# A gated attention block on one core: modulation weights in row pieces after x, v's scale through DRAM, k projected before q

## The chip, the core and the metric

One core of a Trainium2 chip runs the whole kernel. The metric is the device time of one launch in microseconds, as the median of the runs. The engines are TensorE (PE, with its weight loads PEld), VectorE (DVE), ScalarE (ACT), GpSimd (POOL) and SyncE (SP), which only issues transfers here.

## What is computed

```python
mod = c @ w_ada + b_ada                       # shift, scale, gate: 3 x 1024
h = rmsnorm(x, norm_g) * (1 + scale) + shift  # x is 1024 x 1024 float32
proj = h @ w_in                               # q, k, v, z of A and of B, forget logits, two gates
y_a = stick_breaking(q_a, k_a, v_a)           # 8 heads of 64
y_b = forgetting_attention(q_b, k_b, v_b, F)  # 8 heads of 64, F = cumsum(log_sigmoid(f))
y = g0 * ((y_a * silu(z_a)) @ w_o_sb) + g1 * ((y_b * silu(z_b)) @ w_o_fox)
out = rmsnorm(x + gate * (y @ w_out), final_g)
```

## The kernel before

Every float32 product is made of three fp32r matmuls on a high and a low part (`mm3`, lines 181 to 183). A value is split into the two parts by `split` (line 163): ScalarE copies the high part (L165) and VectorE, or GpSimd for some, subtracts it (L166).

**The start** (lines 196 to 332). A list of tokens, `SEQ`, gives the program order: X loads a tile of 128 rows of x, L loads modulation weights, R loads a weight of the first four projections, s squares a tile of x, n makes the inverse norms, x scales and transposes a tile (a tile in `DIAG` is scaled by a matmul with a diagonal matrix, the others by VectorE; `CPY` says who evacuates each bank), a weighs the modulation weights with c (`weigh`), f turns them into the factors of one group of 128 channels (`factors`), m modulates and splits that group (`modulate`), w splits a weight, p projects that group into seven accumulators: two halves of q, of k and of a gate, and one half of z. A scheduler orders each engine's instructions when the program is built, with `SEQ` as the priority, so the order on an engine isn't always that of the list. `load_ada` loads, for a channel group, all 1024 rows of 128 columns of shift and of scale (256 for groups 3 and 4), so a row of a transfer has 512 bytes, and one piece is enough for `factors` of its group. The buffers `ada1`, `ada1b` and `xb1` are reused, `xb1` after x has left it. The splits of the four first weights subtract on GpSimd (`POOLW`).

**The attention stages.** Pairs p = 0 to 7 have two heads each (0 to 3 mixer A, 4 to 7 mixer B), j = 0, 1. `attention(p, j)` runs 12 ticks over row blocks: scores (L623, L625 with `kx`, a copy of k with high and low part swapped that GpSimd's queue moves by DMA, L404 and L405), logits (L701, L708, L713), exponentials (ACT), a DMA transpose of the weights (L663), then products with v (L756, L757) into one `pv` bank that VectorE reduces (L765) and GpSimd scales (L766). Score tiles and the small transposes (`tp_tile`) share one ring of four banks. In mixer B, GpSimd also masks the diagonal block of the bias (L696) before L713 reads it.

**The filler.** Between these, PE gets the projections still needed, as units of 8 steps of three matmuls (v units in steps of six narrower ones). `plan[p, 0]` and `plan[p, 1]` list the units for the two heads of pair p: z of p, gates, v of the next two pairs, and `proj_qk(p + 1)`, q first and then k. `sprinkle` calls small jobs after a counted number of steps. `residual_gate` (18 jobs, one every six steps over pairs 4 and 5) loads and weighs the remaining third of `w_ada` on VectorE (L599).

**v's scale.** For each two pairs of v, `largest` transposes the maxima of the 128 partitions on PE (L467), takes the maximum and makes two powers of two on one partition (L469 to L475); `spread` broadcasts them with a small matmul (L480) and copies them out (L482); `take_v` scales v to 16-bit parts. `forget_gates` (L571) transposes the forget logits through a ring bank at the end of `plan[2, 0]`.

Of the kernel before, what the change touches and what calls it, by code (L numbers as in the profile page):

```python
# [18 lines left out]
P = 128  # L19
# [10 lines left out]
FP = 2  # L30
PEK = ()
EVACS = "k0 z0 g0 g1 q0 k1 q1"
# [4 lines left out]
POOLX = ()  # L37
DIAG = (1, 4, 6)
POOLW = (0, 1, 2, 3)
BATCH = (4,)  # L40
CPY = "dd aa aa aa ad dd ad aa"
GROUPS = ((0,), (1,), (2,), (3, 4), (5,), (6,), (7,))
ADATAG = ("ada1", "ada1b", "ada1", "ada2", "xb1", "ada1b", "ada1")
SEQ = "X2 L0 X0 s0 X1 X3 X4 s3 a0 X7 s2 X6 X5 s1 n0 x0 L1 s4 s5 s7 s6 R0 L2 x2 f0 R2 L3 n1 x1 a3 a1 x3 x4 R1 w0 x5 f1 x7 x6 R3 m0l w1l L6 w1r m0r m1l m1r a2 w3l L5 w2 f2 a5 f3 m2 m3l a6 p0l p1l f4 p0r w3r p1r m3r f5 p2l L7 f6 m4 m5l p2r p3l p3r a7 f7 m6 m5r m7l p4 p5 p6l p6r m7r p7"
WPOOL = ()
# [12 lines left out]
PVAT = (18, 16, 14, 10)  # L58
PVFIRST = 12
TURNAT = (22, 20, 18, 14)  # L60
# [8 lines left out]
def tile_hybrid_block(ctx, tc, x, c, w_ada, b_ada, norm_g, w_in, b_forget,  # L69
# [19 lines left out]
    vd = [dram.tile([P, S], F32, name=f"vd{i}") for i in range(8)]  # L89

    fd = dram.tile([8, S], F32, name="fd")
    gated = dram.tile([1, D], F32, name="gated")
# [5 lines left out]
    def tp_tile():  # L98
        return ps_z.tile([P, 512], F32, name="tp", tag="ps")
# [59 lines left out]
    def load_raw(src, shape, name="wraw"):  # L159
        raw = wpool.tile(shape, F32, name=name, tag="wraw", bufs=3)  # L160
        nc.sync.dma_start(raw, src)
        return raw

    def split(hi, lo, raw, pool=False):
        nc.scalar.copy(hi, raw)  # L165
        (nc.gpsimd if pool else nc.vector).tensor_sub(lo, raw, hi)  # L166
        return hi, lo
# [29 lines left out]
    with tc.tile_pool(name="start", bufs=1) as sp:  # L197
# [4 lines left out]
        half = {"": slice(0, S), "l": slice(0, 512), "r": slice(512, S)}  # L202
        group = {k: g for g in GROUPS for k in g}
        edges = (0,) + BATCH + (TB,)
# [6 lines left out]

        def load_ada(k):
            n = len(group[k]) * P
            tag = ADATAG[GROUPS.index(group[k])]
            ada = sp.tile([P, KB, 2, n], F32, name="ada", tag=tag, bufs=1)
            for j in range(2):
                nc.sync.dma_start(ada[:, :, j, :],
                                  wada[:, j * D + k * P: j * D + k * P + n].rearrange("(q p) n -> p q n", p=P))
            adas[k] = ada

# [51 lines left out]

        def weigh(k):

            n = len(group[k]) * P
            if k in PEK:
                return
            o = ams[k] = sp.tile([P, 2, n], F32, name="am", tag="am%d" % n, bufs=2)
            nc.vector.tensor_scalar(o, adas[k][:, 0], cT[:, 0:1], None, ALU.mult)
            for q in range(1, KB):  # L280
                nc.vector.scalar_tensor_tensor(o, adas[k][:, q], cT[:, q:q + 1], o, ALU.mult, ALU.add)

        def factors(k):
            k0 = group[k][0]
            pm = acc_tile(2)
            for j in range(2):
                if k in PEK:
                    for q in range(KB):
                        nc.tensor.matmul(pm[:, j:j + 1], adas[k][:, q, j, :], cT[:, q:q + 1], start=q == 0,
                                         stop=q == KB - 1)  # L290
                    continue
                nc.tensor.matmul(pm[:, j:j + 1], ams[k0][:, j, (k - k0) * P:(k - k0 + 1) * P], ones,
                                 start=True, stop=True)
            nc.vector.tensor_add(ashf[:, k:k + 1], pm[:, 0:1], b_shift[:, k:k + 1])
            nc.vector.scalar_tensor_tensor(amul[:, k:k + 1], pm[:, 1:2], b_scale1[:, k:k + 1], gT[:, k:k + 1],
                                           ALU.add, ALU.mult)
# [152 lines left out]
    def qcol(p):  # L449
        return (QA if p < 4 else QB) + (p % 4) * P  # L450

    def proj_qk(p):
        return proj(qcol(p), evac_q, p) + proj(qcol(p) + 512, evac_k, p)

# [4 lines left out]
    vmost = {}  # L459
    ones_row = rows[0:1, :]  # L460
    nc.vector.memset(ones_row, 1.0)

    def largest(p):


        pt = tp_tile()
        nc.tensor.transpose(pt[0:1, :P], vmost[p], ident)  # L467
        top = at.tile([1, 1], F32, name="vtop", tag="vtop", bufs=2)
        nc.vector.tensor_reduce(top, pt[0:1, :P], mybir.AxisListType.X, ALU.max)  # L469
        nc.vector.tensor_scalar(top, top, 1e-25, None, ALU.max)  # L470
        e = top.bitcast(I32)
        nc.vector.tensor_scalar(e, e, 0x7F800000, None, ALU.bitwise_and)
        pair = vscale[p] = at.tile([1, 2], F32, name="vpow", tag="vpow", bufs=2)
        nc.vector.tensor_scalar(pair[:, 0:1].bitcast(I32), e, -1.0, float((254 + VSCALE) << 23), ALU.mult, ALU.add)
        nc.vector.tensor_scalar(pair[:, 1:2].bitcast(I32), e, 1.0, float((VSCALE + 15) << 23), ALU.mult, ALU.subtract)  # L475

    def spread(p):

        pt = tp_tile()
        nc.tensor.matmul(pt[:, 0:2], ones_row, vscale[p], start=True, stop=True)  # L480
        o = at.tile([P, 2], F32, name="vsc", tag="vsc", bufs=2)
        nc.vector.tensor_copy(o, pt[:, 0:2])  # L482
        for q in (p, p + 1):
            vscale[q], vback[q] = o[:, 0:1], o[:, 1:2]
# [66 lines left out]
    def load_v(p):  # L551
        vraw[p] = load_raw(vd[p], [P, S], "vraw").rearrange("p (a b d) -> p a b d", a=TB, b=2)
# [16 lines left out]
    def forget_gates():  # L569
        pt = tp_tile()  # L570
        nc.tensor.transpose(pt[:64, :P], fT[0].rearrange("p h a -> p (h a)"), ident)  # L571
# [422 lines left out]
    first_v = proj_v(0)  # L994
    first_v[0].preload()
    def start_evacs():
# [25 lines left out]
    gs = [proj_g(j) for j in list(range(9, 16)) + list(range(8))]  # L1022
    plan = {}
    for p in range(7):
        a, b = [], []
        if p == 0:
            g = sprinkle(gs.pop(0), [(6, lambda: load_v(0)), (8, lambda: largest(0)), (10, lambda: spread(0)),
                                     (13, lambda: take_v(0))])
            a += first_v + g
            vunit[0] = g[1]  # L1030
        else:
            a += proj_z(p)
            zunit[p] = a[-1]
        for _ in range(GSH[p][0]):
            a += gs.pop(0)
        if p % 2:
            a += proj_v(p + 1)
        if p == 2:
            a.append(once(forget_gates))
        b += proj_qk(p + 1)  # L1040
        q = p + 1
        marks = [(14, lambda q=q: largest(q)), (19, lambda q=q: spread(q))] if p % 2 else []
        sprinkle(b, [(12, lambda q=q: load_v(q))] + marks + [(24, lambda q=q: take_v(q))])
        if p == 6:
            a += b[:2]
            b[:2] = []
            b += proj_z(7)
            zunit[7] = b[-1]
        for _ in range(GSH[p][1]):
            b += gs.pop(0)  # L1050
        plan[p, 0], plan[p, 1] = a, b
# [97 lines left out]
```

## Time and profile before

| | |
|---|---|
| device time, 3 runs | 942.94, 944.57, 949.04 us; median 944.57 |
| profiled execution | 944.57 us, of which the span of the core is 942.9 us |
| PE busy | 891.2 us (95% of the span) |
| DVE busy | 704.8 us (75%) |
| ACT busy | 598.3 us (63%) |
| POOL busy | 115.8 us (12%) |
| moved by DMA | 152.14 MB, mean 161 GB/s |

Busy time is taken from one execution. Spans of matmuls overlap, so the distance from one start to the next is what a matmul costs. In a timeline, a bracket holds the idle time of the engine ahead of the row and what ended it. "PEclk" in a table by stretches is the clock granted to TensorE as a share of full speed (2.4 GHz); 0.5 is the lower level.

### The profile page before, as it was taken

Reading aid. Unit: us, or ns where it says so; the run is one execution under the profiler, and the core shown is the slowest. Engines: PE = TensorE matmul, PEld = TensorE weight load, DVE = VectorE, ACT = ScalarE, POOL = GpSimd, SP = SyncE. Lnnn points to the kernel's source line nnn. Section 1 sums busy time; section 2 is a strip of 40 time slices with the busy share of each in tenths; the row PEclk is TensorE's granted clock in tenths of the full one; section 3 lists DMA queues with packets and bytes.
Section 4 is the critical chain, followed back from the end, with each engine's and each line's share of the span. In section 5 each row is a group of like instructions: output and inputs, shape, how many; then the busy total and the mean of one; then the engine's idle time right before and its main releaser. Section 6 shows DMA issues by size and latency. Waiting matters only on the chain. (4 is left out here: it accounts for less than half of the span.)

```text
span 942.9 us, 14905 instructions
## 1 busy us (share of the span) xinstructions
PE 891.2 (95%) x5282; PEld 753.0 (80%) x5282; DVE 704.8 (75%) x1402; ACT 598.3 (63%) x1102; POOL 115.8 (12%) x191
## 2 busy tenths in 40 slices
PE   2799999999999989999999999999999999999997
PEld 2688978889788868889878787897887777788886
DVE  4984998688786788878798768657687767776544
ACT  5656787776777697897678765445667456553222
POOL 0401001000010000100000112211212212540000
PEclk9999999999999989999999999999999999999999
DMA  9933495544594564936548697967999999552221
GB/s 313 305 98 101 100 225 122 127 104 121 132 193 121 143 152 112 176 82 133 147 121 187 175 211 157 210 160 188 192 203 173 279 263 213 201 178 90 101 92 54
DMA packets 260659, 152.14 MB, mean 161 GB/s; under 512 B 157156, under 2 KB 241748, under 8 KB 260584
## 3 DMA queue, kind: packets, MB, share of 16 engines
q1 hardware_dynamic: 257592, 142.78, 60.5%
q0 software_dynamic: 2880, 8.39, 4.9%
q8 instruction: 41, 0.67, 0.3%
q14 instruction: 34, 0.28, 0.1%
q10 hardware_dynamic: 112, 0.02, 0.0%
HBM read 80.31 MB, written 24.71 MB: 111 GB/s over the span
## 5 line engine op out<-in xcount | busy, mean ns | idle before, releaser
L181 PE MATMUL acc<-hhi,w 128*128 128x512 f32 x584 | 237.4, 406 | 0.0
L183 PE MATMUL acc<-hhi,w 128*128 128x512 f32 x584 | 230.0, 394 | 0.0
L182 PE MATMUL acc<-hlo,w 128*128 128x512 f32 x584 | 229.7, 393 | 0.0
L183 PEld LDWEIGHTS acc<-hhi,w 128*128 128x128 f32 x584 | 110.8, 190 | 24.6
L726 DVE SCALAR_TENSOR_TENSOR pc<-pw,pc 128x1024 f16<-128x1024 f32 (+7 forms) x128 | 96.6, 758 | 43.2 <-ACT pc L722 42.4
L181 PEld LDWEIGHTS acc<-hhi,w 128*128 128x128 f32 x584 | 111.4, 191 | 21.7 <-issue 2.0
L182 PEld LDWEIGHTS acc<-hlo,w 128*128 128x128 f32 x584 | 111.3, 191 | 19.6
L722 ACT ACTIVATE pc<-pw 128x1024 f16<-128x1024 f32 (+7 forms) x128 | 86.8, 679 | 19.2 <-DMA wT<-pc 17.8
L718 ACT ACTIVATE pw<-pw,low 128x1024 f32<-128x1024 f32 (+3 forms) x64 | 49.6, 776 | 73.3 <-DVE low L713 73.3
L766 POOL TENSOR_TENSOR ysb<-ysb,fac 128x128 f32<-128x128 f32 x64 | 35.6, 556 | 452.1 <-DVE ysb L765 388.1
L720 ACT ACTIVATE pw<-pw,low 128x1024 f32<-128x1024 f32 (+3 forms) x64 | 49.5, 774 | 62.1 <-DVE low L713 61.7
L530 PE MATMUL acc<-wv,hhi 128*128 128x256 f32 (+1 forms) x256 | 73.6, 288 | 0.0
L532 PE MATMUL acc<-wv,hlo 128*128 128x256 f32 (+1 forms) x256 | 72.4, 283 | 0.0
L531 PE MATMUL acc<-wv,hhi 128*128 128x256 f32 (+1 forms) x256 | 72.4, 283 | 0.0
L701 DVE SCALAR_TENSOR_TENSOR pw<-z,pw 128x512 f32<-128x512 f32 (+4 forms) x96 | 52.9, 553 | 23.1 <-ACT pw L692 22.6
L756 PE MATMUL pv<-vv,wT 128*128 128x128 f16 x534 | 66.6, 220 | 3.7 <-DVE ysb L765 3.7
L623 PE MATMUL z<-ks,qs 128*128 128x512 f32 (+1 forms) x192 | 66.4, 346 | 2.7 <-DVE yT L778 2.7
L625 PE MATMUL z<-kx,qs 128*128 128x512 f32 (+1 forms) x192 | 65.7, 344 | 3.4 <-DMA kx<-ks 3.4
L757 PE MATMUL pv<-vv,wT 128*128 128x128 f16 x534 | 66.5, 220 | 0.0
L166 DVE TENSOR_TENSOR w<-wraw,w 128x1024 fp32r<-128x1024 f32 x44 | 54.0, 1227 | 10.0 <-ACT w L165 8.8
L757 PEld LDWEIGHTS <-wT 128*128 128x128 f16 x576 | 56.6, 98 | 4.4 <-issue 4.1
L708 DVE TENSOR_TENSOR_SCAN pw<-pw 128x512 f32<-128x512 f32 (+2 forms) x64 | 58.9, 921 | 1.2
(276 smaller groups left out, 1985.8 us busy)
## 6 DMA issues: line engine op xcount, KB each, us to landing
wraw<-in_w_in_dram SPq DMA_DIRECT2D x48, 512.0 KB, 4.7
gd<-stg SPq DMA_DIRECT2D x32, 256.0 KB, 2.6
kx<-ks POOLq DMA_DIRECT2D x28, 256.0 KB, 6.4
ada<-in_w_ada_dram SPq DMA_DIRECT2D x12, 512.0 KB, 7.6
zd<-stg SPq DMA_DIRECT2D x16, 256.0 KB, 2.8
zt<-zd SPq DMA_DIRECT2D x32, 128.0 KB, 2.7
vraw<-vd SPq DMA_DIRECT2D x8, 512.0 KB, 3.9
fb<-fd SPq DMA_DIRECT2D x8, 512.0 KB, 4.6
```

The source lines that it names most:

```text
L181: nc.tensor.matmul(ps, w[0], x[0], start=first, stop=False)
L182: nc.tensor.matmul(ps, w[0], x[1], start=False, stop=False)
L183: nc.tensor.matmul(ps, w[1], x[0], start=False, stop=last)
L530: nc.tensor.matmul(ps[:, a], hhi[k][:, t], hi[:, k, :], start=k == 0, stop=False)
L531: nc.tensor.matmul(ps[:, a], hhi[k][:, t], lo[:, k, :], start=False, stop=False)
L532: nc.tensor.matmul(ps[:, a], hlo[k][:, t], hi[:, k, :], start=False, stop=k == KB - 1)
L623: nc.tensor.matmul(o, qs[p, j][:, tq], ks[p, j][:, s], start=True, stop=False)
L625: nc.tensor.matmul(o, qs[p, j][:, tq], kx[p, j][:, s], start=False, stop=not mask)
L722: nc.scalar.activation(pair.parts(a)[0], w, AF.Copy, scale=WSCALE)
L726: nc.vector.scalar_tensor_tensor(lo, pair.logits(a), WSCALE, hi, ALU.mult, ALU.subtract)
L756: nc.tensor.matmul(y[:, a, :], w[:, b + s, :], v, start=s == 0, stop=False)
L757: nc.tensor.matmul(y[:, a, :], w[:, b + nb + s, :], v, start=False, stop=s == nb - 1)
```

## The change

Modulation weights are loaded in eight pieces of 256 rows and 512 columns of shift and of scale (rows of 2048 bytes), four pieces per half of the channels, through three buffers of one tag, all behind the eight tiles of x; `weigh` adds two row groups of 1024 elements per piece, and `factors` of a group needs the four pieces of its half. Five tiles of x instead of three are scaled by a diagonal matmul, fourteen of sixteen transposed banks instead of ten are evacuated by ScalarE, and the four first weight splits subtract on VectorE instead of GpSimd. The splits of v's first weights are put behind the start's last split. v's maxima go through DRAM: GpSimd's queue writes 128 values and reads them back as a row on every partition, and VectorE then makes the powers on all partitions. k is projected ahead of q; the z of pairs 5 and 6 moves from the first half of its own pair to the second half of pair 4 and of pair 5; the first half of pair 6 is left with k of pair 7 and the v jobs, and its second half holds q of pair 7 and, as before, z of pair 7. The forget logits are transposed through the `pv` bank at step 42 of 64.

```diff
-DIAG = (1, 4, 6)
-POOLW = (0, 1, 2, 3)
+DIAG = (1, 4, 5, 6, 7)
+POOLW = ()
-CPY = "dd aa aa aa ad dd ad aa"
-GROUPS = ((0,), (1,), (2,), (3, 4), (5,), (6,), (7,))
-ADATAG = ("ada1", "ada1b", "ada1", "ada2", "xb1", "ada1b", "ada1")
-SEQ = "X2 L0 X0 s0 X1 X3 X4 s3 a0 X7 s2 X6 X5 s1 n0 x0 L1 s4 s5 s7 s6 R0 L2 x2 f0 R2 L3 n1 x1 a3 a1 x3 x4 R1 w0 x5 f1 x7 x6 R3 m0l w1l L6 w1r m0r m1l m1r a2 w3l L5 w2 f2 a5 f3 m2 m3l a6 p0l p1l f4 p0r w3r p1r m3r f5 p2l L7 f6 m4 m5l p2r p3l p3r a7 f7 m6 m5r m7l p4 p5 p6l p6r m7r p7"
+CPY = "dd aa aa aa aa aa aa aa"
+SEQ = "X2 X0 s0 X1 X3 X4 s3 X7 s2 X6 X5 s1 L0 L1 n0 x0 L2 s4 s5 s7 s6 a0 x2 L3 R0 n1 x1 a1 x3 x4 R1 a2 L4 w0 x5 x7 x6 a3 R2 L5 f0 m0l w1l f1 w1r m0r m1l m1r f2 R3 a4 L6 w2 f3 m2 m3l w3l p0l p1l a5 L7 p0r w3r p1r m3r p2l a6 a7 f4 f5 p2r p3l p3r f6 f7 m4 m5l m6 m5r m7l p4 p5 p6l p6r m7r p7"
-PVFIRST = 12
+PVFIRST = 13
...
+    vm = [dram.tile([1, P], F32, name=f"vm{i}") for i in range(4)]
...
+        def load_ada(i):
+
+            ada = adas[i] = sp.tile([P, 2, 2, 512], F32, name="ada", tag="ada", bufs=3)
+            rows_ = wada[i % 4 * 2 * P:(i % 4 + 1) * 2 * P, :]
             for j in range(2):
+                c0 = j * D + i // 4 * 512
+                nc.sync.dma_start(ada[:, :, j, :], rows_[:, c0:c0 + 512].rearrange("(q p) n -> p q n", p=P))
...
+        def weigh(i):
+
+            g = i // 4
+            if i % 4 == 0:
+                ams[g] = sp.tile([P, 2, 512], F32, name="am", tag="am", bufs=2)
+            for x in range(2):
+                q = i % 4 * 2 + x
+                if q == 0:
+                    nc.vector.tensor_scalar(ams[g], adas[i][:, x], cT[:, 0:1], None, ALU.mult)
+                else:
+                    nc.vector.scalar_tensor_tensor(ams[g], adas[i][:, x], cT[:, q:q + 1], ams[g], ALU.mult, ALU.add)
...
-        return proj(qcol(p), evac_q, p) + proj(qcol(p) + 512, evac_k, p)
+        return proj(qcol(p) + 512, evac_k, p) + proj(qcol(p), evac_q, p)
...
     def largest(p):
...
+        nc.gpsimd.dma_start(vm[p // 2].rearrange("o p -> p o"), vmost[p])
+        every = vscale[p] = at.tile([P, P], F32, name="vev", tag="vev")
+        nc.gpsimd.dma_start(every, vm[p // 2].to_broadcast((P, P)))
+
+    def spread(p):
...
+        o = at.tile([P, 3], F32, name="vsc", tag="vsc", bufs=2)
+        top = o[:, 2:3]
+        nc.vector.tensor_reduce(top, vscale[p], mybir.AxisListType.X, ALU.max)
...
     def forget_gates():
-        pt = tp_tile()
+        pt = pv_tile()
...
-    first_v[0].preload()
+    with tc.issue_after(last_split[0].ins), tc.issue_after(last_split[1].ins):
+        first_v[0].preload()
...
-            g = sprinkle(gs.pop(0), [(6, lambda: load_v(0)), (8, lambda: largest(0)), (10, lambda: spread(0)),
-                                     (13, lambda: take_v(0))])
+            g = sprinkle(gs.pop(0), [(4, lambda: load_v(0)), (5, lambda: largest(0)), (13, lambda: spread(0)),
+                                     (14, lambda: take_v(0))])
...
-        else:
-            a += proj_z(p)
-            zunit[p] = a[-1]
+        elif p < 5:
+            a += project_z(p)
...
-            a.append(once(forget_gates))
-        b += proj_qk(p + 1)
+            sprinkle(a, [(42, forget_gates)])
+        if p < 6:
+            b += proj_qk(p + 1)
+        else:
+            qk = proj_qk(7)
+            a += qk[:2]
+            b += qk[2:]
         q = p + 1
-        marks = [(14, lambda q=q: largest(q)), (19, lambda q=q: spread(q))] if p % 2 else []
-        sprinkle(b, [(12, lambda q=q: load_v(q))] + marks + [(24, lambda q=q: take_v(q))])
-        if p == 6:
-            a += b[:2]
-            b[:2] = []
-            b += proj_z(7)
-            zunit[7] = b[-1]
+        marks = [(6, lambda q=q: largest(q)), (20, lambda q=q: spread(q))] if p % 2 else []
+        sprinkle(b if p < 6 else a, marks + [(12 if p < 6 else 5, lambda q=q: load_v(q)), (24 if p < 6 else 14, lambda q=q: take_v(q))])
+        for x in {4: (5,), 5: (6,), 6: (7,)}.get(p, ()):
+            b += project_z(x)
```

## Rows read from the trace of the kernel before

**Rows 1.** The page: span, and busy time and share by engine.

```profile
span 942.9 us, 14905 instructions
...
PE 891.2 (95%) x5282; PEld 753.0 (80%) x5282; DVE 704.8 (75%) x1402; ACT 598.3 (63%) x1102; POOL 115.8 (12%) x191
```

**Rows 2.** Waits, whole span: waiter <- releaser, total us, times, longest.

```profile
PE acc L292 <- DVE am L281: 7.3, 3, 4.5
...
PE tp L480 <- DVE vpow L475: 4.1, 3, 2.2
...
PE pv L756 <- DVE ysb L765: 3.7, 2, 2.0
...
PE z L625 <- DMA kx<-ks: 3.4, 1, 3.4
...
PE z L623 <- DVE yT L778: 2.7, 1, 2.7
...
DVE pw L713 <- POOL fb L696: 4.0, 8, 1.9
```

**Rows 3.** Stretches: length; busy PE, PEld, DVE, ACT, POOL; PEclk; DMA share; GB/s.

```profile
42.20:79.00 36.80, 36.80 (x167) 30.75 (x168) 25.99 (x53) 17.14 (x22) 1.85 (x1) 0.95 0.41 102
...
340.00:350.00 10.00, 7.15 (x51) 5.74 (x49) 8.96 (x19) 8.58 (x20) 0.65 (x1) 0.83 0.65 184
350.00:360.00 10.00, 10.00 (x38) 7.83 (x38) 5.00 (x12) 8.81 (x19) 0.00 (x0) 0.82 0.74 152
...
556.00:591.00 35.00, 30.39 (x191) 25.32 (x189) 26.88 (x51) 19.15 (x34) 7.61 (x15) 1.00 0.79 168
...
590.00:600.00 10.00, 8.52 (x48) 7.17 (x49) 4.43 (x13) 2.62 (x8) 1.45 (x4) 0.83 1.17 255
...
667.00:697.00 30.00, 30.00 (x195) 25.71 (x195) 22.02 (x54) 19.71 (x37) 5.61 (x14) 1.00 0.98 213
```

**Rows 4.** Timeline of PE, the start: start us, us, instruction, idle before.

```profile
30.96 0.48 PE L181 MATMUL z<-hhi,wqk 128*128 128x512 f32 x1
...
42.18 0.61 PE L292 MATMUL acc<-ones,am 128*128 128x1 f32 x4 [2.21 <-DVE am L281]
...
48.90 0.50 PE L292 MATMUL acc<-ones,am 128*128 128x1 f32 x4
49.26 0.48 PE L181 MATMUL pv<-hhi,w 128*128 128x512 f32 x1
...
70.20 0.39 PE L181 MATMUL z<-hhi,wqk 128*128 128x512 f32 x1
...
79.04 0.39 PE L181 MATMUL acc<-hhi,w 128*128 128x512 f32 x1
```

**Rows 5.** Transfers at 8 to 16 us (x), then 16 to 26 us (weights).

```profile
DMA packets 897, 3.28 MB, mean 410 GB/s; under 512 B 96, under 2 KB 96, under 8 KB 897
...
DMA packets 5634, 2.96 MB, mean 296 GB/s; under 512 B 96, under 2 KB 5599, under 8 KB 5634
```

**Rows 6.** DVE's groups by shape: start (first three), whole span (last).

```profile
L281 DVE SCALAR_TENSOR_TENSOR am<-ada,cols,am 128x256 f32<-128x256 f32 x42 | 20.9, 518 | 0.5
...
L281 DVE SCALAR_TENSOR_TENSOR am<-ada,cols,am 128x512 f32<-128x512 f32 x7 | 7.2, 1022 | 0.1
...
L259 DVE TENSOR_SCALAR diag<-ident,inv 128x128 f32<-128x128 f32 x3 | 3.0, 984 | 0.0
...
L599 DVE SCALAR_TENSOR_TENSOR gacc<-wraw,cols,gacc 128x1024 f32<-128x1024 f32 x7 | 9.0, 1282 | 10.7 <-DMA wraw<-in_w_ada_dram 10.7
```

**Rows 7.** Tile kx, all its transfers from GpSimd's queue.

```profile
DMA to landing us min/median/max: 2.2/5.1/8.8
```

**Rows 8.** Timeline of PE at three idle times of the attention stages.

```profile
347.18 0.58 PE L623 MATMUL z<-ks,qs 128*128 128x256 f32 x1 [2.67 <-DVE yT L778]
...
566.78 0.22 PE L756 MATMUL pv<-vv,wT 128*128 128x128 f16 x1 [1.74 <-DVE ysb L765]
...
591.48 0.47 PE L625 MATMUL z<-kx,qs 128*128 128x512 f32 x1 [3.35 <-DMA kx<-ks]
```

More of the change, by code (lines that the diff above doesn't have):

```diff
@@ L30 @@
 FP = 2
-PEK = ()
 EVACS = "k0 z0 g0 g1 q0 k1 q1"
@@ L162, in load_raw @@
         return raw
+    last_split = []
     def split(hi, lo, raw, pool=False):
-        nc.scalar.copy(hi, raw)
-        (nc.gpsimd if pool else nc.vector).tensor_sub(lo, raw, hi)
+        last_split[:] = [nc.scalar.copy(hi, raw), (nc.gpsimd if pool else nc.vector).tensor_sub(lo, raw, hi)]
         return hi, lo
@@ L202, in tile_hybrid_block @@
         half = {"": slice(0, S), "l": slice(0, 512), "r": slice(512, S)}
-        group = {k: g for g in GROUPS for k in g}
         edges = (0,) + BATCH + (TB,)
@@ L210, in load_x @@
             nc.sync.dma_start(xt[t], x2[t * P:(t + 1) * P, :])
[L212 to L215, printed above, removed]
+        def load_ada(i):
+            ada = adas[i] = sp.tile([P, 2, 2, 512], F32, name="ada", tag="ada", bufs=3)
+            rows_ = wada[i % 4 * 2 * P:(i % 4 + 1) * 2 * P, :]
             for j in range(2):
-                nc.sync.dma_start(ada[:, :, j, :],
-                                  wada[:, j * D + k * P: j * D + k * P + n].rearrange("(q p) n -> p q n", p=P))
-            adas[k] = ada
+                c0 = j * D + i // 4 * 512
+                nc.sync.dma_start(ada[:, :, j, :], rows_[:, c0:c0 + 512].rearrange("(q p) n -> p q n", p=P))
         def load_w0(i):
@@ L271, in turn_x @@
                 copy(xnT[:, 4 * b:4 * b + 4, t * P:(t + 1) * P], pt.rearrange("p (a b) -> p a b", a=4))
[L273 to L281, printed above, removed]
+        def weigh(i):
[8 more added lines that the diff above has]
+                    nc.vector.scalar_tensor_tensor(ams[g], adas[i][:, x], cT[:, q:q + 1], ams[g], ALU.mult, ALU.add)
         def factors(k):
-            k0 = group[k][0]
             pm = acc_tile(2)
             for j in range(2):
[L287 to L292, printed above, removed]
+                nc.tensor.matmul(pm[:, j:j + 1], ams[k // 4][:, j, k % 4 * P:(k % 4 + 1) * P], ones,
                                  start=True, stop=True)
@@ L459, in tile_hybrid_block @@
     vmost = {}
-    ones_row = rows[0:1, :]
-    nc.vector.memset(ones_row, 1.0)
     def largest(p):
-        pt = tp_tile()
-        nc.tensor.transpose(pt[0:1, :P], vmost[p], ident)
-        top = at.tile([1, 1], F32, name="vtop", tag="vtop", bufs=2)
-        nc.vector.tensor_reduce(top, pt[0:1, :P], mybir.AxisListType.X, ALU.max)
+        nc.gpsimd.dma_start(vm[p // 2].rearrange("o p -> p o"), vmost[p])
[5 more added lines that the diff above has]
+        nc.vector.tensor_reduce(top, vscale[p], mybir.AxisListType.X, ALU.max)
         nc.vector.tensor_scalar(top, top, 1e-25, None, ALU.max)
@@ L472, in largest @@
         nc.vector.tensor_scalar(e, e, 0x7F800000, None, ALU.bitwise_and)
[L473 to L482, printed above, removed]
+        nc.vector.tensor_scalar(o[:, 0:1].bitcast(I32), e, -1.0, float((254 + VSCALE) << 23), ALU.mult, ALU.add)
+        nc.vector.tensor_scalar(o[:, 1:2].bitcast(I32), e, 1.0, float((VSCALE + 15) << 23), ALU.mult, ALU.subtract)
         for q in (p, p + 1):
@@ L569, in forget_gates @@
     def forget_gates():
-        pt = tp_tile()
+        pt = pv_tile()
         nc.tensor.transpose(pt[:64, :P], fT[0].rearrange("p h a -> p (h a)"), ident)
@@ L1023, in tile_hybrid_block, with project_z @@
     plan = {}
+    def project_z(p):
+        units = proj_z(p)
+        zunit[p] = units[-1]
+        return units
     for p in range(7):
```

## The prediction

> **What bounds the kernel now.** I read the page first. PE is busy 891.2 of 942.9 us, DVE 704.8, ACT 598.3 [rows 1], so TensorE sets the time, and a change can only win where PE stands still or runs at its lower clock. The list of waits, cut to PE, says where: at L292 for the modulation sums (7.3 us, of which 2.2 at 40 us), at L480 for v's powers (4.1), at L756 for the reduction of the single `pv` bank (3.7), at L625 for `kx` (3.4), at L623 for a bank of the score ring (2.7) [rows 2]. The table by stretches adds the second price of a stall: behind those at 347 and 591 us the granted clock is 0.82 to 0.83 over ten microseconds [rows 3, 8]; at half speed that costs 10 x (0.17 + 0.18) = 3.5 us behind the first and 10 x 0.17 = 1.7 us behind the other. Last the start's timeline: from 42.18 us on PE never stops until the first projections end at 79 us, and before that it did little of them [rows 3, 4].
>
> **The start: -5.5 us.** The seven accumulators need 7 x 8 x 3 = 168 matmuls. Their distance is (79.04 - 70.20) / 39 = 0.227 us [rows 4], so 38.1 us in all. Behind 42.2 us stand 143 of them: the stretch has 167 records, 24 of these from six factor groups [rows 3]. Only 25 ran between 30.96 and 42.2, since channel groups came one by one. Where they run without a break, the end is first matmul + 38.1 + eight factor groups of 49.26 - 48.90 = 0.36 [rows 4], 2.9, + one spell of the low clock as now, 0.05 x 36.8 = 1.8 [rows 3]: first + 42.8.
>
> When can the first one run? x moves at 410 GB/s, weights in rows of 512 bytes at 296 [rows 5]; rows of 2048 bytes are not in the trace. I bound them by these two and take the middle, 350, as they lie between both in length. Without the 1.05 MB of modulation weights that now go in among x, its last tile lands some 1.05/0.35 = 3 us earlier than the 16 us at which that rate changes [rows 5]: 13 us. Four pieces (4.19 MB) take 12.0, so 25.0. Behind the last come two sums of 1024 elements, 1.28 each by the nearest row of that shape (L599) [rows 6], then matmul, factors, modulation and split, for which I estimate 3.1: 30.7 us. The first half of the channels then gives 84 matmuls: 84 x 0.227 + 1.4 + 1.8 = 22.3 us of work, to 53.0. The second half needs another 4.19 MB at 350 and 2.1 MB of first weights at 296: 25.0 + 12.0 + 7.1 + 5.7 = 49.8. No gap, and the end is 30.7 + 42.8 = 73.5 against 79.0: -5.5. At 410 for the pieces it is 71.7 (-7.3), at 296 75.7 (-3.3). I keep 0 as the upper end, since the scheduler may order DVE otherwise.
>
> DVE has room. The weighing is 56 instructions now (eight per loaded group), 20.9 + 7.2 us in its two main forms; sixteen of 1.28 are 20.5 [rows 6]. The four subtractions that come over from GpSimd cost about as much each (5.1), and the wider instructions pay for them. DVE also shows slow spells while GpSimd subtracts: a diagonal matrix of 128 elements takes 0.98 us in the mean, where a sum of 256 elements takes 0.52 [rows 6]. Page "SBUF — State Buffer" of the Trainium skill (section "Who interferes with whom") says that a GpSimd instruction and a DVE one with two SBUF inputs block each other whole; by that rule the slow spells go with `POOLW`. The trace fits it, and no term of the sum rests on it. More copies and casts on ACT lie beside PE's 38 us of matmuls; without that cover four copies would be some 2 us. The splits of v's first weights move behind the last split, which should now be done about ten microseconds before PE ends; without that slack they are four passes, some 5 us late.
>
> **v's scale: -4.1 + 1.5.** The two PE steps per pair of pairs and their wait go: -4.1 [rows 2], at best that and at worst nothing, if PE meets the same late DVE at the next `pv` or score bank. New is a chain on GpSimd's queue: a write, its landing, a read, its landing, then six small DVE instructions in place of six. Nearest for a landing is kx's from the same queue: 2.2 to 8.8, median 5.1 [rows 7]. Two make 10.2 (4.4 to 17.6). The cover is 8 steps at pair 0 and 14 later; a step is three matmuls, 0.68 us, and with attention's share about 0.9: 7 us and 13 us. So the median is 3 us late once and in time three times. DVE would stand there and ACT's scaling of v behind it; PE sees part: I take +1.5. The ends are 0 and (17.6 - 7) + 3 x (17.6 - 13) = +24. Behind the write, GpSimd's queue also holds the diagonal masks of mixer B and the scaling of `ysb`; L713 waits for masks 4.0 us in all today [rows 2], once in the change (pair 5) that could grow by a landing, which is inside the 24.
>
> **k before q: -5.1.** The 3.35 us at 591.48 go [rows 8], for `kx` now has q's 16 steps (and z's 16) between its transfer and its use, 11 us or more against a landing of 8.8 at most [rows 7]; with the clock's 1.7 that makes 5.1. Next in line is q, which needs no transfer. At worst the clock falls elsewhere: -3.4.
>
> **z one stage earlier: -1.7 + 3.0.** The second half of pair 4 (556 to 591 us) has 32 steps and PE idles 4.6 us in it; 1.74 of that is the `pv` wait at 566.78 [rows 3, 8]. It gets 48 steps, which should cover that (0 to -3.6, of which I take the 1.7). The steps come from the first halves of pairs 5 and 6. The latter (667 to 697 us) now has PE full for 30.0 us, DVE 22.0, ACT 19.7 [rows 3]. With 16 of 32 steps gone PE needs 30.0 - 10.9 = 19.1. DVE loses two gate multiplications per half of z and a split, some 4 us: 18.0. In the stretch at 556 DVE got through 26.9 us in 35.0, a share of 0.77 [rows 3]; at that share 18.0 takes 23.4 and PE idles 4.3. The ends are 0 and 4.3; I take 3.0, nearer the second, for this is the same kind of stage with a thin filler.
>
> **Forget logits: -4.6.** At 344 to 347 us PE waits 2.85 for ring banks (10 - 7.15) [rows 3], 2.67 of it for a bank that the late L778 holds [rows 8]. The job leaves the ring, so the next score tile gets another bank, and at step 42 of 64 no product with v is due. -2.85, and of the clock's 3.5 I take half. Ends -6.4 and 0. `PVFIRST` one tick later costs nothing: filler covers it, or one tick of about 3 us if not.
>
> **Sum.** -5.5 - 4.1 + 1.5 - 5.1 - 1.7 + 3.0 - 4.6 = -16.5. The profiled execution took 944.57 us and is the median run itself, with a span of 942.9; 944.57 - 16.5 = **928.1 us**.
>
> **Rivals.**
> 1. *The start wins, the middle gives back.* DVE at 75% [rows 1] is why the powers, the `pv` reduction and L778 were late; take one wait away and PE meets the next. For it: three of the four waits behind the start name DVE [rows 2]. Against: they are few, and PE is full for long stretches between. Then only the start, `kx` and the added costs count: -5.5 - 5.1 + 4.5 = -6.1, 938.5 us.
> 2. *The start wins nothing.* Nothing can be projected until four pieces have come; if DVE weighs them late, the second half starts PE again from a stop. For it: PE's longest wait in the start is for DVE's sums already [rows 2]. Against: the bytes per microsecond only rise. 928.1 + 5.5 = 933.6 us.
> 3. *Slower: the trip through DRAM.* DVE takes its instructions in order, so a late row of maxima holds everything behind it, four times. At the top of kx's landings the overrun is 24 us [rows 7]: 944.57 - 16.5 - 1.5 + 24 = 950.6 us. It decides from an overrun of 18 us on, that is with landings of about 8 us in the mean ((18 + 7 + 3 x 13) / 8). Against: these are 512 bytes and 64 KB, where kx is 256 KB. Page "SBUF — State Buffer" (section "SBUF: two separate sides") warns that DVE in its two-port modes keeps GpSimd from writing descriptors for its transfers; by that rule the landings go to the long end. The spread of kx's landings [rows 7] leaves room for it, and no row separates it from full queues.
>
> **How the numbers follow.** The forecast gets 0.58, rival 1 0.20, rival 2 0.14, rival 3 0.08. About 1% (9.4 us) is what a measurement of this kernel tells from no change: faster means below 935.1, slower above 954.0. Faster: 0.9 of the forecast (0.52), 0.7 of rival 2 (0.10), a quarter of rival 1 (0.05): 0.67. Slower: of rival 3, whose tail goes beyond its 950.6, and mishaps of order, 0.06. The rest, 0.27, is within 1%. The forecast's own range is 921 to 935. The sum of all good ends, -7.3 - 4.1 - 5.1 - 3.6 - 6.4, is 918; upward the range takes in rival 1 and half the way to rival 3: 918 to 943.
>
> **What would show it.** Right: first projection matmul near 31 us, the last of the 168 near 73 to 74, no idle time of more than a microsecond between; no wait of PE for powers, for `kx` or at the forget transpose; some 3 us of idle PE in the first half of pair 6, and a short wait of DVE for the row of maxima at pair 0. Wrong: the start ending at 77 or later; DVE waiting several microseconds for that row each time; PE's total idle time as before with other names, which is rival 1.

## The result, and the profile after

The changed kernel takes 982.34 us in the median (978.01 to 983.28, four runs) beside 943.76 for the kernel before (942.94 to 949.04): a ratio of 1.0384, interval 1.0350 to 1.0418. The forecast was 928.1 us. The profiled execution took 983.28 us, with a span of 981.4.

The page of the changed kernel, which answers to [rows 1]:

```profile
span 981.4 us, 14888 instructions
...
PE 907.1 (92%) x5286; PEld 762.7 (78%) x5286; DVE 693.5 (71%) x1359; ACT 599.0 (61%) x1106; POOL 105.2 (11%) x193
```

The span is 38.5 us longer and splits in two. TensorE is idle for 981.4 - 907.1 = 74.3 us, where it was 942.9 - 891.2 = 51.7: 22.6 us more. And it is busy 15.9 us longer with four instructions more: the same work at the lower clock, by the mean granted clock of 0.969 (before 0.990). VectorE has less work than before, ScalarE as much.

The waits of the changed kernel over the whole span (waiter, releaser, total us, times, longest), which answer to [rows 2]:

```profile
DVE vsc L467 <- DMA vev<-vm: 40.1, 4, 13.0
...
ACT vv L548 <- DVE vsc L471: 20.6, 3, 11.1
...
POOL vev L460 <- DMA vm<-vmx: 18.5, 2, 10.2
PE pv L746 <- DVE ysb L755: 17.1, 5, 4.5
```

The first line is the largest new wait of VectorE: four times it stands at the row of maxima that comes back from DRAM, 10 us on average, and what it would have done next comes late. ScalarE's scaling of v waits behind it, and TensorE's wait for the `pv` bank rises from 3.7 to 17.1 us. The waits for v's powers (L480) and for `kx` (L625) are gone, as forecast.

The two transfers of the trip, by their lines in the changed kernel (first the write of 128 maxima, then the broadcast read):

```profile
L458 POOL DMA_DIRECT2D vm<-vmx x4: 582/607/609, 116.6 to 656.7; - x4
...
DMA to landing us min/median/max: 9.0/9.8/10.5
```

```profile
L460 POOL DMA_DIRECT2D vev<-vm x4: 552/556/592, 127.3 to 666.0; - x4
...
DMA to landing us min/median/max: 3.4/4.0/6.6
```

And the timeline of VectorE at the first and the last of the four trips:

```profile
131.15 0.29 DVE L467 TENSOR_REDUCE vsc<-vev 128x1 f32<-128x128 f32 x1 [9.27 <-DMA vev<-vm]
...
672.61 0.28 DVE L467 TENSOR_REDUCE vsc<-vev 128x1 f32<-128x128 f32 x1 [13.05 <-DMA vev<-vm]
```

From the issue of the write (116.6) to the reduction (131.15) pass 14.6 us. VectorE had other work for at most 14.6 - 9.3 = 5.3 of them (1.4 of these it waited for ScalarE); in the last trip, 656.7 to 672.61, for 2.9 of 15.9.

What the standstill costs beyond itself shows in a table of stretches (length; busy time of PE, PEld, DVE, ACT and POOL; PEclk; DMA share; GB/s): around the trips in pairs 0 and 3, TensorE runs at 0.72 and 0.63 of its clock.

```profile
130.00:136.00 6.00, 3.82 (x10) 2.82 (x11) 4.85 (x12) 3.62 (x8) 0.00 (x0) 0.72 0.34 62
...
498.00:512.00 14.00, 7.14 (x29) 5.76 (x30) 12.72 (x26) 8.90 (x13) 2.53 (x5) 0.63 0.53 117
```

The start ends where it did. TensorE's timeline shows the first projection matmul at 35.55 us, and the one that stands at 79.04 in [rows 4] at 78.75:

```profile
35.55 1.63 PE L181 MATMUL z<-hhi,wqk 128*128 128x512 f32 x3
...
78.75 0.39 PE L181 MATMUL acc<-hhi,w 128*128 128x512 f32 x1
```

### The profile page after: what moved, and what is told of

Read it like the earlier page. It is cut to its first block, busy times and chain, and to the rows that moved or that the text cites. A ratio compares the mean times of both kernels' runs of the same rounds, so it can differ in the third digit from the quotient of the medians.

```text
span 981.4 us, 14888 instructions
## 1 busy us (share of the span) xinstructions
PE 907.1 (92%) x5286; PEld 762.7 (78%) x5286; DVE 693.5 (71%) x1359; ACT 599.0 (61%) x1106; POOL 105.2 (11%) x193
## 5 line engine op out<-in xcount | busy, mean ns | idle before, releaser
L183 PEld LDWEIGHTS acc<-hhi,w 128*128 128x128 f32 x584 | 112.0, 192 | 25.0
L181 PEld LDWEIGHTS acc<-hhi,w 128*128 128x128 f32 x584 | 113.2, 194 | 22.9 <-issue 2.5
L746 PE MATMUL pv<-vv,wT 128*128 128x128 f16 x534 | 69.6, 225 | 22.8 <-DVE ysb L755 17.1
L747 PEld LDWEIGHTS <-wT 128*128 128x128 f16 x576 | 58.0, 101 | 21.0 <-issue 20.8
L756 POOL TENSOR_TENSOR ysb<-ysb,fac 128x128 f32<-128x128 f32 x64 | 32.3, 505 | 390.4 <-DVE ysb L755 350.4
L747 PE MATMUL pv<-vv,wT 128*128 128x128 f16 x534 | 69.6, 225 | 0.0
L746 PEld LDWEIGHTS <-wT 128*128 128x128 f16 x576 | 57.4, 101 | 7.8 <-DMA wT<-pc 3.6
L166 DVE TENSOR_TENSOR w<-wraw,w 128x1024 fp32r<-128x1024 f32 (+2 forms) x46 | 55.3, 1203 | 6.5 <-ACT w L166 6.5
```

What stands on the lines that cost most here:

```text
L181: nc.tensor.matmul(ps, w[0], x[0], start=first, stop=False)
L183: nc.tensor.matmul(ps, w[1], x[0], start=False, stop=last)
L746: nc.tensor.matmul(y[:, a, :], w[:, b + s, :], v, start=s == 0, stop=False)
L747: nc.tensor.matmul(y[:, a, :], w[:, b + nb + s, :], v, start=False, stop=s == nb - 1)
```

## The experiments

Two theories. T, on which the first four runs (e1 to e4) were laid out: the wait makes the loss, VectorE in its order behind a trip longer than its cover. W, which came from their result: the write itself, 128 elements of 4 bytes, is slow and holds up the transfers beside it. Ratios are to runs of the kernel before on the same chip, with their 95% intervals.

**Without the trip.** e1 is the changed kernel with v's scale on TensorE again (`largest` and `spread` as before, at the changed step counts).

```diff
-        nc.gpsimd.dma_start(vm[p // 2].rearrange("o p -> p o"), vmost[p])
+        nc.tensor.transpose(pt[0:1, :P], vmost[p], ident)
...
+        nc.tensor.matmul(pt[:, 0:2], ones_row, vscale[p], start=True, stop=True)
```

> The changed kernel with v's scale made on PE as in the kernel before (transpose and small matmul; the jobs stay at the changed step counts); all the rest of the change stays. Theory T (the trip through DRAM is the loss): the four waits of VectorE for the row of maxima (40.1 us in all) go, and with them the longer stages they fall in, 42.3 + 64.3 + 63.5 + 39.0 + 51.2 us against 40.8 + 54.7 + 56.0 + 35.1 + (33.5 + 10.9) before, that is some 29 us: 950 to 956 us. Rival R (the new order of k, q, z and the forget job is the loss, and the trip only sits in idle time): less than 10 us better than the changed kernel, 972 or more.

Measured: 951.36 us, 1.0068 (1.0048 to 1.0089). That is in the range of theory T. So some 30 of the 38.5 us belong to the trip, and the other parts, which were to bring 13.9 us, cost 6.

**The trip alone.** e2 is the kernel before with the trip and the changed step counts:

```diff
-        nc.tensor.transpose(pt[0:1, :P], vmost[p], ident)
+        nc.gpsimd.dma_start(vm[p // 2].rearrange("o p -> p o"), vmost[p])
+        nc.gpsimd.dma_start(every, vm[p // 2].to_broadcast((P, P)))
```

> The kernel before with v's scale through DRAM alone (with the changed step counts of its jobs). Theory T: slower than before by about the same sum, 25 to 35 us, 969 to 979 us, with four waits of VectorE of 8 to 13 us each for the row of maxima and the write landing after 9 to 10.5 us. Rival R: within 10 us of before, 945 to 954 us.

Measured: 985.42 us, 1.0415 (1.0381 to 1.0449), over the range: the trip by itself makes the whole loss.

**The trip read late.** e4 is the changed kernel with the write at step 1 and the reduction at step 28 (14 in pair 0), held behind the VectorE work of those steps.

```diff
-        marks = [(6, lambda q=q: largest(q)), (20, lambda q=q: spread(q))] if p % 2 else []
+        marks = [(1, lambda q=q: largest(q))] if p % 2 else []
+        late = [(28, lambda q=q: spread(q)), (30, lambda q=q: take_v(q))] if p % 2 else [(24 if p < 6 else 14, lambda q=q: take_v(q))]
```

> The changed kernel with the trip kept but given more cover: the write at step 1 instead of 5 or 6, the scale at step 28 instead of 20 (14 instead of 13 for pair 0), take_v at 30 (15), and the five scale instructions pinned on VectorE behind the logits traced just before them. On VectorE 17 to 23 instructions now stand between the last maximum and the row's use, where it was 8 to 10 (pair 0 stays at 10). Theory T (the loss is VectorE standing in order at the row): the three waits behind pair 0 fall from 30.8 us to under 6, pair 0 keeps some 9, and the time falls by 15 to 22 us, to 960 to 967 us. Rival Q (the queue of GpSimd held by the two transfers is the loss): the time stays within 5 us of the changed kernel, 977 or more.

Measured: 970.29 us, 1.0265 (1.0235 to 1.0295), above the range. VectorE's wait for the row fell from 40.1 to 8.7 us, yet only 12 us came back, where theory T had 15 to 22. ScalarE's timeline says what else is late, a weight load beside the write:

```profile
263.68 1.05 ACT L166 CAST w<-wraw 128x1024 fp32r<-128x1024 f32 x1 [9.73 <-DMA wraw<-in_w_in_dram]
```

**The write alone, read by nobody.** This tells W from T: the kernel before, with TensorE's turn and powers kept, and one line added.

```diff
     def largest(p):
+        nc.gpsimd.dma_start(vm[p // 2].rearrange("o p -> p o"), vmost[p])
         pt = tp_tile()
```

> Kernel before with one thing added: at the four places where the row maxima are turned, GpSimd's queue also writes them to DRAM, 128 elements of 4 bytes, one from each partition. Nobody reads them. Theory W (the write itself holds up other transfers beside it): the weight and v loads that fall into it land after 8 to 11 us in place of 3.9 and 4.7, and the time is 948 to 960 us against some 945 of before. Theory T (only the wait for the trip costs, VectorE in order behind it): no transfer is late and the time is that of before within 1 us. By either theory the write lands after 8 to 11 us; if it lands after 2 to 4 us, its length in the changed kernel came from the traffic beside it.

Measured: 966.9 us, 1.0221 (1.0189 to 1.0252): 21 us for a write that nothing waits for. Theory W holds, and its range was too low. The transfers at 225 to 262 us (KB each, median us to landing), first in the kernel before:

```profile
wraw<-in_w_in_dram SPq DMA_DIRECT2D x4, 512.0 KB, 6.1
...
vraw<-vd SPq DMA_DIRECT2D x1, 512.0 KB, 4.6
...
wT<-pc SPq DMA_TRANSPOSE x4, 4.5
```

and in e5:

```profile
wraw<-in_w_in_dram SPq DMA_DIRECT2D x3, 512.0 KB, 10.8
...
vraw<-vd SPq DMA_DIRECT2D x1, 512.0 KB, 9.2
...
wT<-pc SPq DMA_TRANSPOSE x4, 6.8
vm<-vmx POOLq DMA_DIRECT2D x1, 0.5 KB, 9.1
```

Weights, v and the transposed weights all land late. The write that lands after 9.1 us was issued at 245.84. A table of short stretches of e5 shows the end of its time and what follows:

```profile
252.00:254.00 2.00, 2.00 (x18) 1.58 (x17) 0.00 (x0) 0.00 (x0) 0.00 (x0) 1.00 0.82 37
254.00:256.00 2.00, 2.00 (x23) 1.79 (x21) 0.00 (x0) 0.00 (x0) 0.00 (x0) 1.00 0.53 42
...
258.00:260.00 2.00, 0.00 (x0) 0.00 (x0) 1.53 (x4) 1.94 (x4) 0.00 (x0) 1.00 0.44 115
```

The DMA engines are busy for 0.82 and 0.53 of the time and move 37 and 42 GB/s (257 at 248 to 250 us). ScalarE and VectorE stand (ScalarE waits 6.9 us for that weight load, VectorE 6.0 for ScalarE), TensorE uses up what it had, and from 257 us on it stands too.

**Queue or form?** e9 issues the same unread write on SyncE's queue (`nc.sync` for `nc.gpsimd`). e10 leaves it on GpSimd's, but writes one row:

```diff
+        line = stage()[0:1, 0:P]
+        nc.vector.tensor_copy(line, pt[0:1, :P])
+        nc.gpsimd.dma_start(vm[p // 2], line)
```

> Kernel before with the unread write of 128 elements of 4 bytes, as in run e5 (1.0221 times before), but issued on SyncE's queue in place of GpSimd's. If the 128 small pieces make the write slow: it lands after 6 us or more, holds up the same loads, and the time is 950 us or more (against some 945.5 of before). If it was GpSimd's queue that made it slow: it lands after 2 to 3 us and the time is 944 to 948 us.

> Kernel before with an unread write on GpSimd's queue as in run e5, but of one row: VectorE copies the turned maxima to SBUF, and the write is one run of 512 bytes. If the 128 small pieces were the cost: it lands after 2 to 4 us, no load beside it is late, and the time is that of before, or up to 2 us over it for the four added copies in VectorE's order (944 to 948 us). If any write on GpSimd's queue at this place costs: 955 to 967 us, as e5.

Measured: e9 969.43 us, 1.0266 (1.0233 to 1.0300); e10 945.9 us, 1.0005 (0.9988 to 1.0023). It is the form, not the queue. It isn't the moment either: the four row writes are issued between 120.5 and 647.8 us, those of e5 between 117.3 and 648.3. What in the form makes it slow these runs don't separate, for the two differ in the size of a piece (4 bytes or a run of 512) and in the number of partitions that it comes from (128 or 1). The number of pieces alone is not enough: the broadcast read puts a row of 512 bytes on each of 128 partitions and lands after 3.3 to 4.2 us in e6 (below). Nor do the packets that the profile lists tell the two apart: 32 for the write of 128 elements in e5 and 32 for the row in e10, each on GpSimd's queue, while e9 has 576 more than the kernel before for its four writes on SyncE's, 144 each, and lands as late as e5.

The waits of e9 show the path from late loads to TensorE: ScalarE waits 30.1 us for weights (6.6 before, 21.4 in e5, 7.2 in e10), VectorE behind it, and TensorE 23.3 us for v's powers (4.1 in [rows 2]), although their own computation is unchanged. The kernel before, then e9:

```profile
ACT w L165 <- DMA wraw<-in_w_in_dram: 6.6, 4, 2.4
```

```profile
ACT w L166 <- DMA wraw<-in_w_in_dram: 30.1, 5, 9.1
...
PE tp L481 <- DVE vpow L476: 23.3, 4, 12.3
```

The two writes as they land, in e9 and in e10:

```profile
DMA to landing us min/median/max: 8.9/9.5/10.1
```

```profile
DMA to landing us min/median/max: 3.6/3.8/4.7
```

**The trip with a row.** e6 is e4 with the write in e10's form, issued at step 14 (8 in pair 0):

```diff
-        marks = [(1, lambda q=q: largest(q))] if p % 2 else []
+        marks = [(14, lambda q=q: largest(q))] if p % 2 else []
```

> The kernel of run e4 (trip through DRAM read late, 28 and 14 steps in) with the write in another form: the maxima are turned to one row by TensorE, copied by VectorE, and written as one run of 512 bytes from one partition (step 14; step 8 in pair 0). Theory W (128 pieces of 4 bytes make the write long and hold up what is beside it): the write lands after 2 to 3 us, the weight loads beside it land in about 4.7 us, and the time is 948 to 955 us, that of run e1. Theory T (it was the late place of the scale, or the read, that cost e4 its 20 us over e1): 965 to 972 us, as e4.

Measured: 956.6 us, 1.0116 (1.0088 to 1.0144): 14 us under e4, 5 over e1, a little over the range. The write lands after 3.0 to 5.6 us. The edit moves the write as well as reshaping it, so e6 by itself doesn't part form from place; e5 and e10 do. A trip in good form and read late costs about 5 us more than what it replaces, which is the small matmul and the powers on one partition: the turn on TensorE stays. VectorE still waits 6.7 us for it.

**The other parts, one at a time**, on the kernel before: e3 has the new start (without the pinned load of v's weights and without `PVFIRST = 13`), e7 the forget logits in `pv`'s bank at step 42, e8 the order of k, q and z. The core of each:

```diff
+            ada = adas[i] = sp.tile([P, 2, 2, 512], F32, name="ada", tag="ada", bufs=3)
...
-            a.append(once(forget_gates))
+            sprinkle(a, [(42, forget_gates)])
...
-        return proj(qcol(p), evac_q, p) + proj(qcol(p) + 512, evac_k, p)
+        return proj(qcol(p) + 512, evac_k, p) + proj(qcol(p), evac_q, p)
```

> The kernel before with the new start alone (pieces of the modulation weights behind x, five diagonal tiles, ScalarE copies, no GpSimd subtractions, the new token list). The forecast's step said -5.5 us, 938 us. Theory S (the first projection matmul comes at 35.6 us and at the low clock, since the splits of the first weights and the one bank of the factors stand between the last sum and it): the projections end at 77 to 78 us instead of 79, and the time is 0 to 1.5 us under before, 942.5 to 944.5 us.

> Kernel before with the forget logits' transpose in pv's bank at step 42 and nothing else changed. The prediction counted 4.6 us for it: then 940 to 942 us. The changed kernel has a wait of 4.74 us at this transpose, a low-clock spell behind it and a stage (2,0) 3.2 us longer: then it is 945 to 949 us.

> Kernel before with the order of the projections of the changed kernel alone (k ahead of q, z of pairs 5, 6 and 7 in the stage before); start, scale of v and forget logits as before. The prediction counted -5.1 -1.7 +3.0 = -3.8 us: then some 941 us and no wait for the last correction of k. If the four waits of 3.4 us that go come back elsewhere: 944 to 946 us.

Measured: e3 947.44 us, 1.0023 (1.0005 to 1.0041); e7 945.08, 1.0000 (0.9980 to 1.0021); e8 947.01, 1.0011 (0.9994 to 1.0027). None brings anything; e3 and e8 are above their ranges. Two of them did remove what they aimed at. In e8 the `kx` wait is gone, and the second stage of pair 7 begins at 762.8 us (763.8 before). In e7 the stage with the forget job takes 58.3 us in place of 60.4. Both lose it again. e7 does so at once, in the second stage of pair 3, which takes 59.0 us in place of 56.0 (59.6 to 60.0 in e14, e16 and e17, which have the same change). That stage, in the kernel before and in e7:

```profile
464.23:520.25 56.02, 53.82 (x301) 44.21 (x299) 47.81 (x90) 45.03 (x84) 4.01 (x8) 1.00 0.67 156
```

```profile
463.54:522.57 59.03, 55.39 (x300) 45.40 (x299) 48.80 (x92) 47.02 (x88) 4.00 (x8) 0.97 0.69 151
```

TensorE's wait for v's powers in it is 3.6 us in place of 2.2, and the clock falls to 0.97. e8 loses it later: from the start of its second stage of pair 7 it has 182.8 us left (before 179.1; e7 180.2). Part of that lies behind 796 us; the same stretch of the kernel before, of e7, and of e16 (below):

```profile
796.00:808.00 12.00, 9.61 (x68) 7.15 (x66) 7.49 (x14) 10.53 (x15) 3.95 (x3) 1.00 0.93 295
```

```profile
796.00:808.00 12.00, 9.64 (x61) 6.96 (x60) 5.04 (x12) 10.17 (x16) 2.72 (x2) 0.86 1.08 307
```

```profile
796.00:808.00 12.00, 10.55 (x63) 7.64 (x60) 7.53 (x13) 9.23 (x12) 0.80 (x2) 1.00 1.06 260
```

TensorE's idle time there is alike before and in e7, some 2.4 us; but before it kept its clock, and in e7 the clock fell for 12 x 0.14 x 2 = 3.4 us. But each of these tables is one execution. The granted clock of the kernel before lies between 0.985 and 0.993 over its runs, and the median is 0.9905 for e7 and for e16 alike. So that an edit moved a spell of this size isn't shown.

**The parts together.** e11 is the changed kernel with v's scale on TensorE at the step counts of before; e13 is e11 with the forget job of before, e14 with the start of before, e15 with z's places of before, and e18 without the two small parts of the start that e3 lacked. Two of these edits:

```diff
-        marks = [(6, lambda q=q: largest(q)), (20, lambda q=q: spread(q))] if p % 2 else []
+        marks = [(14, lambda q=q: largest(q)), (19, lambda q=q: spread(q))] if p % 2 else []
...
-    with tc.issue_after(last_split[0].ins), tc.issue_after(last_split[1].ins):
-        first_v[0].preload()
+    first_v[0].preload()
```

> The changed kernel with v's scale on TensorE at the step counts that before has (8 and 10 in pair 0, 14 and 19 later); run e1 had it at the changed step counts and took 1.0068 times before, with TensorE waiting 6.07 us for the row maxima. If these counts were what cost e1 its 6 us: 944 to 947 us. If the start, the order of k and z and the forget logits cost it together: 950 us and more. By the prediction's own terms without v's scale (-5.5 -5.1 -1.7 +3.0 -4.6) it would be 931 us.

> Run e11 (all of the change but v's scale, 1.0065) without the change of the forget logits. If the forget logits are what the other parts don't bear: 944 to 947 us, and the second stage of pair 6 back to some 27 us. If the start or the moves of z are: 950 us or more.

> Run e11 with the start of before: k first, z moved, forget logits changed. If the start is what turns the sum (it shifts all that follows by about 1 us and no more): 944 to 947 us, and the second stage of pair 6 at some 27 us. If k and z with the forget logits are: 950 us or more.

> Run e11 with z of pairs 5 to 7 and the order of pair 6 as before: new start, k first, forget logits. If the moves of z make the loss in the second stage of pair 6 (a wait for a transposed block behind the transfers of that stage): that wait is gone and the time is 942 to 946 us. If not: 950 us or more.

> Run e11 (1.0065) without two small parts of the start: the load of pair 0's v weights is no longer pinned behind the last split, and the first sum over v stays at step 12. If these two cost: 944 to 947 us (the 1.0023 of e3 or less). If the pieces and the norm's order themselves cost: 949 us and more.

Measured: e11 951.73 us, 1.0065 (1.0039 to 1.0091); e13 950.8, 1.0070 (1.0049 to 1.0092); e14 944.34, 1.0000 (0.9986 to 1.0013); e15 950.45, 1.0043 (1.0019 to 1.0066); e18 952.49, 1.0078 (1.0056 to 1.0100). The step counts are cleared, and so are the forget job and the two small parts. Without the start the 6 us are gone, and it costs more in company than alone. Whether the moves of z have a share is open: the intervals of e15 and e11 overlap. In e11, e13 and e18 the loss shows in the second stage of pair 6, some 600 us later, which takes 33.7, 33.8 and 35.9 us, beside 26.5 before, 26.4 in e14 and 27.3 in e15. So in these traces it takes the start and z's moves together. TensorE's timeline of e18 has there

```profile
707.24 0.29 PE L747 MATMUL pv<-vv,wT 128*128 128x128 f16 x1 [6.09 <-DMA wT<-pc]
```

with 6.8 us of half clock beside it. In e14 that wait is 2.0 us; e15 has none there and is slow all the same in the median, though its trace is of a quick execution (947.19 us beside 950.45). How the start reaches so far is not settled.

**A version that wins?** e12 and e17 are e11 and e14, e16 is e7, each with the low part of y of pair 5 on VectorE:

```diff
-        yg[p] = split(hi, lo, load_raw(yd[p], [P, S]) if raw is None else raw, p > 3 and p % 2 == 1)
+        yg[p] = split(hi, lo, load_raw(yd[p], [P, S]) if raw is None else raw)
```

> Run e11 with one more change: the low part of y of pair 5, which GpSimd takes 2.37 us for while TensorE waits 1.25 us for it (at 801.9 us in the kernel before), on VectorE, which takes some 1.4 us. TensorE sits idle for 2.2 of 4 us there, and in e8 a stretch of 6.8 us at half clock begins there. If that gap brings the clock down: no low stretch near 800 us and the time is 1 to 4 us under e11. If not: within 1 us of e11, or over it where VectorE is then the later one.

> Run e7 (kernel before with the forget logits changed, 1.0000; its stage of that job was 2.1 us shorter, and 6.8 us of half clock came at 802.6 us that were not there before) with the low part of y of pair 5 on VectorE in place of GpSimd, so that TensorE's wait of 1.25 us at that place goes. If the half-clock stretch there comes from that gap: it is gone and the time is 941 to 944 us, 2 to 4 us under the kernel before. If not: 945 us.

> Run e14 (kernel before with k first, z moved, forget logits changed: 1.0000, with 6.8 us of half clock from 801.0 us) with the low part of y of pair 5 on VectorE. If that half-clock stretch goes with the wait, as it did from e7 to e16: 940 to 942 us, under the kernel before. If another one takes its place: 943 to 945 us.

Measured: e12 950.75 us, 1.0058 (1.0038 to 1.0079); e16 943.85, 0.9989 (0.9974 to 1.0003); e17 943.51, 0.9987 (0.9971 to 1.0002). In the traces of e16 and e17 no spell lies between 796 and 808 us; the trace of e7, without that edit, has one of 3.4 us (not the 6.8 of e16's expectation). e16 and e17 beat the changed kernel by 4%; against the kernel before 1 us is all that is left, and both intervals reach 1.

## Why the prediction was wrong

**The step that failed is v's scale (-4.1 + 1.5).** It measured about +30 on top of the other parts and +39 alone (e2). Three things in it were wrong, and rival 3 (0.08) had the first two.
- *The landings.* I took the write's from the rows of kx [rows 7], transfers of 256 KB, and argued in rival 3 that 512 bytes must be shorter. The write took 9.0 to 10.5 us, longer than any of kx's; the read, 64 KB, took 3.4 to 6.6. Bytes were the wrong measure: e9 and e10 move the same 512 bytes in 9.5 and in 3.8 us. The Trainium skill bears on this: page "DMA: Bandwidth & Descriptors", section "Rules for kernel authors", says that a strided last dimension becomes one descriptor per element. The 144 packets of a write in e9 (128 and 16) agree with that; the 32 of a write in e5, as many as for the row, neither show it nor explain the slowness, and I had not weighed the rule. Its section "Anatomy of one DMA — SWDGE (gpsimd) path" fits about 2.0 us plus the bytes for one transfer; by that the write would be an estimated 2.0 us, and the measured 9.0 to 10.5 decide.
- *The cover.* I counted 7 and 13 us of TensorE's steps between write and use. What counts is the work of the engine that waits, in its own order: VectorE had 3 to 5 us of it. The overrun was 40.1 us; rival 3 decides from 18. By rival 3's own sum that would have been 944.57 - 16.5 - 1.5 + 40.1 = 966.7 us, so even it is 16 us short.
- *The traffic.* No term and no rival had a cost for what the write does to other transfers. That is the part that e5 shows alone: 21 us with nobody waiting for the write. It fits that reading later gave back so little in e4.

**The rule that rival 3 takes from the Trainium skill** (page "SBUF — State Buffer", section "SBUF: two separate sides"), on VectorE keeping GpSimd from writing descriptors, does not explain it: e9's write comes from SyncE's queue and is as slow.

**The start (-5.5).** Its end measured -0.3 in the changed kernel, and the whole time +2 us in e3. The pieces came faster than my 350 (381 GB/s over 13 to 24 us), and from the first matmul on the sum held: 35.55 + 42.8 = 78.35, against 78.75, where the matmul behind the 168th starts. The failed term is the first matmul, 30.7 forecast and 35.55 found. VectorE began its sums at 18.08 us and was busy with them and the norm, with a break of 0.7, until 29.97, where I had only the last two behind the last piece; then four groups of factors, waiting 2.5 us for each other in one bank, and the first splits took 5.6 us where I had estimated 3.1. In company the part costs some 6 us, which none of my terms had; it isn't explained.

**k before q (-5.1) and z (-1.7 + 3.0).** Mechanism right, worth nothing: `kx` isn't waited for any more, the second half of pair 4 has TensorE full (35.00 of 35 us at 556 to 591 in e8), yet e8 is at 1.0011. TensorE is idle for 945.6 - 894.0 = 51.6 us in e8, against 51.7 before: between 555 and 700 us it now waits 2.1 us for the `pv` bank and 1.6 for a transposed block, and 1.7 of the stage of pair 6 that lost its filler (677.2 to 699.9 us) are idle, where I had 3.0. That is the sign that the prediction named for rival 1: idle time as before, with other names. The clock's shares in these terms (1.7 for `kx`) didn't come either: the median granted clock is 0.989 in e8 and before. The page of e8, and its waits of TensorE at 555 to 700 us:

```profile
span 945.6 us, 14906 instructions
...
PE 894.0 (95%) x5282; PEld 755.1 (80%) x5282; DVE 705.2 (75%) x1402; ACT 598.0 (63%) x1102; POOL 113.8 (12%) x191
```

```profile
PE pv L756 <- DVE ysb L765: 2.1, 1, 2.1
PE pv L756 <- DMA wT<-pc: 1.6, 1, 1.6
```

**Forget logits (-4.6).** The wait moved rather than went. TensorE's timeline of the changed kernel, for [rows 8]'s 2.67:

```profile
345.26 0.42 PE L561 MATMUL pv<-ident,fT 128*64 128x128 f32 x1 [4.74 <-DVE ysb L755]
```

The bank that I had held to be free at step 42 was still being reduced. In e7 that wait is 2.7, the stage wins 2.1 us, and the second stage of pair 3 gives them back.

**Sum.** By the ratios of e1 and the changed kernel, the parts without the trip came to +6 us in place of -13.9, and the trip on top of them to +30 in place of -2.6. The two don't add up as terms do: alone, the trip costs +39 (e2).

## What to carry to other kernels

Price a small transfer by its form, not by its bytes, and price what it does to the transfers beside it: four writes of the same 512 bytes cost nothing as a row and 21 us as 128 elements of 4 bytes each. Count the cover of a wait on the engine that waits, in its own order, and not on the engine that one hopes to keep busy. Where a kernel is bound by a full TensorE, a stall of 2 to 3 us that is removed may come back under another name, so count the idle time of the whole span, and the granted clock over several executions, before crediting one.

## What the hardware showed unasked

- A write of 128 four-byte elements lands after 8.1 to 10.7 us, from GpSimd's queue and from SyncE's, in e4, e5, e9 and the changed kernel; while it is under way the transfers beside it crawl (37 to 42 GB/s at 252 to 256 us of e5). A row of the same bytes lands after 3.0 to 5.6 us.
- A GpSimd subtraction held up VectorE in the norm, once as far as the trace shows. The 984 ns of [rows 6] are a mean of three diagonal matrices of 279, 280 and 2394 ns, not a slow spell of all. The long one stands beside a subtraction on GpSimd and ends with it (29.62 and 29.54 us). In the changed kernel, where GpSimd does nothing there, each of five takes 280 to 290 ns. The section "Who interferes with whom" (Trainium skill, page "SBUF — State Buffer") agrees in that one blocks the other whole; the two SBUF inputs of the rule as the prediction has it aren't seen, since the held instruction is a scaling of one tensor. The kernel before, its two instructions, then the changed kernel:

```profile
L259 DVE TENSOR_SCALAR diag<-ident,inv x3: 279/280/2394, 19.0 to 27.2; 128x128 f32<-128x128 f32 x3
...
26.76 2.78 POOL L166 TENSOR_TENSOR wqk<-wraw,wqk 128x1024 fp32r<-128x1024 f32 x1 [25.04 <-ACT wqk L165]
...
27.23 2.39 DVE L259 TENSOR_SCALAR diag<-ident,inv 128x128 f32<-128x128 f32 x1
```

```profile
L258 DVE TENSOR_SCALAR diag<-ident,inv x5: 280/282/290, 15.5 to 25.9; 128x128 f32<-128x128 f32 x5
```

- An idle time of some 2.4 us of TensorE between 796 and 808 us left the clock at 1.00 in one execution of the kernel before and went with 0.86 in one of e7.
